# hi and lo of the activation side by side: one 512-column matmul in the transposed projections

## The chip, the cores and the metric

The kernel runs on one core of one Trainium2 chip. The metric is device time in microseconds, from a compiled program that is launched once per measurement. A profile gives one further execution with the start and the length of every instruction. In its rows PE is the TensorE matmul, PEld the weight load of TensorE, DVE the VectorE, ACT the ScalarE, POOL the GpSimd, and SP the SyncE, which here issues most DMAs.

## The reference

The reference is a network of two blocks over 256 tokens of width 1024, in float32. What matters here, cut down:

```python
# first block, layer 0 (even): three attentions over one input projection
qa, ka, va, qb, kb, vb, qm, gate = split_cols(h @ w_in_even[e], SPLIT_EVEN)
...
y = jnp.concatenate([ya, yb, ym], axis=-1) * jax.nn.silu(gate)
x = x + y @ w_out_even[e]
# layer 1 (odd): neighbourhood attention with 16 heads, and memory attention
qc, kc, vc, qm, gate = split_cols(h @ w_in_odd[o], SPLIT_ODD)
...
x = x + y @ w_out_odd[o]
# second block: mixer, cross attention, MLP
x = x + hybrid_mixer(rms_norm(x, g_mix), w_in, conv_w, g_attn_out, g_conv_out, w_out)
x = x + memory_cross_attention(rms_norm(x, g_xattn), rms_norm(mem, g_mem), w_q_mem, w_kv_mem, w_o_mem)
x = x + squared_relu_mlp(rms_norm(x, g_mlp), w_up, w_down)
return rms_norm(x, g_final)
```

Each `h @ w` is a product of 256 x 1024 with 1024 columns in, and between 512 and 4608 columns out. Two of these blocks keep memory keys and values (`mem @ w_kv`) as well.

## The kernel before, in words

**Split products.** Every operand of a large product is split in two float32r halves: hi is the value rounded, lo is the rest. A product is then made as hi·hi + hi·lo + lo·hi, three matmuls that accumulate in PSUM (`mm3`, line 421). For a weight, `split` (line 413) writes hi with a copy on ACT into a buffer `wh`, and lo with a subtraction on DVE into `wl`. Four buffers of each exist.

**Two kinds of projection.** `proj_n` (line 439) leaves the tokens on the partitions: the activation is the stationary operand, the split weight moves with up to 512 columns. `proj_t` (line 427) leaves the output columns on the partitions: 128 columns of the weight are stationary, the activation moves with all 256 tokens. It loads 256 weight columns for all eight k-tiles of 128 rows as one tile, and for each 128 columns (a block `f`) it splits 128 x 1024 weights and does eight times `mm3`. Both blocks of a call lie in one PSUM bank of 512 float32, and the readers read that bank directly.

**The activation.** hi and lo of an activation lie in tiles of [128, 4, 256], two for hi and two for lo, each with four k-tiles. A function `hT(l, k)` gives hi (l = 0) or lo (l = 1) of k-tile k. Four places make them: `gain_t` (line 478, tiles `gh`), `turns` (line 614, tiles `mT`), and in `layer_even` (line 985, tiles `hT`); `proj_n`, `proj_t` and `up_first` (line 1277) read them.

**Who reads a transposed projection.** `gate_tile` (line 769; a tanh on ACT, then a product on DVE), `q_stack` and `k_stack` (lines 649 and 661; halves for the heads), `mem_key` and `hilo` for the memory attention, the convolution in `mixer` (line 1177), the queries in `cross` (line 1238) and the squared relu of the MLP's `up` (line 1271).

**Memory.** Four PSUM banks bear the tag `mm` and four the tag `at`; projections use `mm`, except the MLP's `up` calls, which use `at`, as attention does. In SBUF a pool of 25 slots of 4 KB a partition (`SLOTS`) holds all larger activation tiles; work tiles have tags and counts of their own.

**Order.** The program is recorded first, then a planner orders it with costs per instruction (class `Plan`, `solve` at line 260): it takes, on each engine, the ready instruction that comes first in the program, moved by a few fixed shifts. Every instruction is then issued from line 284, so all rows of the profile name that line, and the tiles tell them apart. Attention heads are not called in place but queued in small steps; `pace` (line 330) lets some of them in after every four k-tiles of a projection, and `flush` does what is left before its result is needed. For a few operations, such as the scaling of softmax rows (`scaled`, line 601), the planner may choose between DVE and ACT.

**Stages.** In order of time: the even layer (normal projections for its keys and rotated queries, then eight and eight heads, and four memory heads), the odd layer (two groups of eight heads, four memory heads), the mixer (eight heads and a convolution), the cross attention (four heads of 256), the MLP (eight slices of 512 hidden columns, `up` of the next slice ahead of `down` of the current one). Keys and values of the second memory (`filling`, line 817) are put between stages.

Of the kernel before, what the change touches and what calls it, by code (L numbers as in the profile page):

```python
# [13 lines left out]
ALU = mybir.AluOpType  # L14
AX = mybir.AxisListType

P = 128
S = 256
D = 1024
KT = D // P  # L20
# [9 lines left out]
class Plan:  # L30
# [5 lines left out]
    class Engine:  # L36

        def __init__(self, plan, name):
            self.plan, self.engine = plan, name
# [244 lines left out]
            f(*[self.real(v) for v in args], **{k: self.real(v) for k, v in kwargs.items()})  # L284


class Kernel:

    def __init__(self, ctx, tc, a, out):
        self.tc, self.nc, self.a, self.out = tc, Plan(tc.nc), a, out  # L290

        class Pool:

            def __init__(pool, name, bufs, space=None):
                pool.space = space
                pool.real = ctx.enter_context(tc.tile_pool(name=name, bufs=bufs, **({"space": space} if space else {})))

            def tile(pool, shape, dtype, tag=None, name=None, bufs=1):
                return self.nc.tile(pool, shape, dtype, tag, name, bufs)

        pool = Pool
        self.base = pool("base", 1)
        self.wp = pool("wp", 4)
        self.wk = pool("wk", 2)
        self.bp = pool("bp", SLOTS)
        self.ps = pool("ps", 2, space=bass.MemoryType.PSUM)
        self.dr = pool("dr", 1, space=bass.MemoryType.DRAM)
        self.n = 0
        self.bg = deque()
        self.credit = 0.0  # L310
        self.rate = 0.0

    def name(self, s):
        self.n += 1
        return f"{s}_{self.n}"
# [4 lines left out]
    def slot(self, shape, name, dtype=F32R):  # L320
        return self.bp.tile(shape, dtype, tag="b4", name=self.name(name), bufs=SLOTS)

# [104 lines left out]
    def proj_t(self, w, c0, hT, n=256, tag="mm"):  # L427

        raw = self.load(w, 0, KT, c0, n)
        po = self.psum(tag)  # L430
        for f in range(n // P):
            wh, wl = self.split(raw[:, :, f * P:(f + 1) * P])
            for k in range(KT):
                self.mm3(po[:, f, :], wh[:, k, :], wl[:, k, :], hT(0, k), hT(1, k), k == 0, k == KT - 1)
                if k % 4 == 3:
                    self.pace()
        return po[:, :n // P, :]

    def proj_n(self, pieces, nk, n, hT, banks=None, start=True, stop=True):

        nc = self.nc
        po = banks or [self.psum("mm", [P, 512]) for _ in range(2)]
        for k0, view in pieces:
            wh, wl = self.split(view)
            for t in range(2):
                ts = slice(t * P, (t + 1) * P)
                for j in range(view.shape[1]):
                    k = k0 + j
                    o = po[t][:, :n]
                    xh, xl = hT(0, k)[:, ts], hT(1, k)[:, ts]  # L450
                    nc.tensor.matmul(o, xh, wh[:, j, :], start=start and k == 0, stop=False)
                    nc.tensor.matmul(o, xh, wl[:, j, :], start=False, stop=False)
                    nc.tensor.matmul(o, xl, wh[:, j, :], start=False, stop=stop and k == nk - 1)
                self.pace()
        return po
# [22 lines left out]
    def gain_t(self, src, key):  # L478

        nc = self.nc  # L480
        tiles = [[self.slot([P, 4, S], "gh") for _ in range(2)] for _ in range(2)]

        def turn(k):
            v, g, h, l = src[k // 4][:, k % 4, :], self.gcol(key, k), f(0, k), f(1, k)
            nc.scalar.activation(h, v, AF.Copy, scale=g)
            nc.vector.scalar_tensor_tensor(l, v, g, h.bitcast(F32), ALU.mult, ALU.subtract)

        f = lambda l, k: tiles[l][k // 4][:, k % 4, :]
        return f, turn

    def spread(self, r, b):

        nc = self.nc
        diag = self.work("p", [P, 2, P], PB)
        pb = self.psum("at")
# [83 lines left out]
    def mem_key(self, h, l, po, m):  # L579

        t = self.work("p", [P, 2, S], PB)
        self.nc.vector.tensor_tensor(t, po, m[2].unsqueeze(1).to_broadcast([P, 2, S]), ALU.mult)
# [23 lines left out]
    def square_sum(self, v, ms):  # L606

        junk = self.work("p", [P, 512], PB)
        self.nc.either(("scalar", "activation", (junk, v, AF.Square), {"scale": 1.0 / 32.0, "accum_out": ms}),
# [4 lines left out]
    def turns(self, tag, halves, key):  # L614

        nc = self.nc
        tiles = [[None, None], [None, None]]

        def turn(c, k2):
            if k2 == 0:  # L620
                for l in range(2):
                    tiles[l][c] = self.slot([P, 4, S], "mT")
            pt = self.psum("at")
            for j in range(2):
                k = 2 * k2 + j
                for t in range(2):
                    nc.tensor.transpose(pt[:, j, t * P:(t + 1) * P], halves[c][:, t, k * P:(k + 1) * P], self.ident)
            for j in range(2):
                k = 2 * k2 + j
                g = self.gcol(key, 4 * c + k)  # L630
                h, l = tiles[0][c][:, k, :], tiles[1][c][:, k, :]
                nc.scalar.activation(h, pt[:, j, :], AF.Copy, scale=g)
                nc.vector.scalar_tensor_tensor(l, pt[:, j, :], g, h.bitcast(F32), ALU.mult, ALU.subtract)

        for c in range(2):
            for k2 in range(2):
                self.later(tag, lambda c=c, k2=k2: turn(c, k2))
        return lambda l, k: tiles[l][k // 4][:, k % 4, :]


    def hilo(self, h, l, po, scale=1.0):
# [63 lines left out]
    def softmax(self, sc, bias=None, sink=None, causal=False):  # L705
# [3 lines left out]
        n = [P, S] if causal else [S, S]  # L709
        p = self.work("p", [P, 2, S], PB)  # L710
        st = self.work("st", [P, 8], 8)
# [39 lines left out]
    def pv_pair(self, ws, vs, causal=False):  # L751
# [4 lines left out]
        for e, ((ph, pl), v) in enumerate(zip(ws, vs)):  # L756
            for k in range(2):
                q = slice(P, S) if causal and k else slice(0, S)
                nc.tensor.matmul(po[:, e, q], v(k), ph[:, k, q], start=k == 0, stop=False)
                nc.tensor.matmul(po[:, e, q], v(k), pl[:, k, q], start=False, stop=k == 1)  # L760
        u = self.work("y", [P, S], YB)
        o = self.work("y", [P, S], YB)
        for e in range(2):
# [16 lines left out]
    def gated(self, y, f, o, g):  # L780
        nc = self.nc
        t = self.work("y", [P, S], YB)
        nc.vector.scalar_tensor_tensor(t, o, 0.5, g[:, f, :], ALU.mult, ALU.mult)
# [124 lines left out]
    def rope(self, tag, po, n, i, rx):  # L908
# [15 lines left out]
        def turn(t):  # L924
            src, r = po[t][:, :n * 64], rs[t]
            z = self.work("p", [P, 8, 64], PB)
            nc.vector.scalar_tensor_tensor(z[:, :n, :], src.rearrange("p (h c) -> p h c", c=64), rx[:, t:t + 1],
# [28 lines left out]
    def layer_even(self):  # L956
        nc, a = self.nc, self.a
# [20 lines left out]
        po = self.proj_n(pieces(), KT, 384, xg)  # L978
# [3 lines left out]
        nc.vector.tensor_tensor(sq[0], sq[0], sq[1], ALU.add)  # L982
        r = self.token_rms(sq[0])
        rb = self.spread(r, self.work("y", [P, S], YB))
        tiles = [[self.slot([P, 4, S], "hT") for _ in range(2)] for _ in range(2)]
        for c in range(2):
            t = self.slot([P, 4, S], "xs", F32)
            for k in range(4):
                nc.vector.scalar_tensor_tensor(t[:, k, :], self.xT[c][:, k, :], self.gcol("norm0", 4 * c + k), rb,
                                               ALU.mult, ALU.mult)  # L990
            for k in (0, 2):
                self.hilo(tiles[0][c][:, k:k + 2], tiles[1][c][:, k:k + 2], t[:, k:k + 2])
        hT = lambda l, k: tiles[l][k // 4][:, k % 4, :]
        self.window_bias()
        vs = []
        for c0 in (128, 256):
# [144 lines left out]
    def token_rms(self, sq):  # L1141

        nc = self.nc
        s = self.work("y", [P, S], YB)
        nc.vector.tensor_reduce(s, sq.rearrange("p r s -> p s r"), AX.X, ALU.add)
# [8 lines left out]
    def mixer(self, hT):  # L1154
# [22 lines left out]
        for i in range(2):  # L1177
# [8 lines left out]
            for f in range(2):  # L1186
                ff = 2 * i + f
                acc = self.work("y", [P, S], YB)
                tap = lambda j: self.gcol("convw", 4 * j + ff)
# [62 lines left out]
    def mlp(self, ms):  # L1252
# [11 lines left out]
        def square(t, f, n, po):  # L1264
            r = self.work("tanh", [P, 2, S], 2)[:, :n]
            nc.scalar.activation(r, po, AF.Relu)
            q = self.work("p", [P, 2, S], PB)[:, :n]
            nc.scalar.activation(q, r, AF.Square)
# [93 lines left out]
BIAS = [40, 80, 110, 0, 0]  # L1362
VERBOSE = False
LAG = (3, 1)
SLOTS = 25
YB = 5
PB = 4
PH = 4
IDLE = [1, 2, 1]
# [79 lines left out]
```

## Time and profile before

| | us |
|---|---|
| median of 3 runs | 787.56 (786.85 to 789.11) |
| the profiled execution | 786.07 |
| its span, first to last instruction | 784.3 |
| PE busy in it | 769.9 |
| DVE busy | 578.2 |
| ACT busy | 506.3 |
| POOL busy | 74.7 |

The mean granted TensorE clock is 0.997 of full speed. How to read the rows: a group's row names engine, operation, the tile written and the tiles read (buffer numbers left out), partitions by elements, a count; after the bar come the busy time of the group in us, the mean length of one in ns, and the idle time of the engine just before them with what ended it. A matmul's length runs to its modelled end in the pipeline, so the lengths of neighbours overlap; busy time counts the overlap once. A row of the waits names the waiting engine and tile, what it waited for, the total in us, the number of times and the longest. The share of 16 DMA engines that the main queue used is 52.0%.

### The profile page before, as it was taken

The page shows a single profiled execution, that of the slowest core. Times are in us where ns is not written, and L with a number is a line of the kernel's source. Part 1 is how long each engine was busy: PE and PEld are TensorE (multiplying, and loading weights), DVE is VectorE, ACT ScalarE, POOL GpSimd, SP SyncE. Part 2 cuts the span into 40 slices and gives each one's busy share as a digit, 9 for nine tenths or more (in the row PEclk, how much of TensorE's full clock was granted, in tenths as well). Part 3 has the DMA queues.
Part 4 walks back from the last instruction along what each step waited for, and adds up shares of the span by engine and source line. Part 5 has one row for each costly group of instructions (what it writes and reads, how often), then busy time and mean ns, then how long its engine had stood idle before and what let it go on. Part 6 is the DMA issues. An engine that isn't in the chain of part 4 may idle for free.

```text
span 784.3 us, 13568 instructions
## 1 busy us (share of the span) xinstructions
PE 769.9 (98%) x5320; PEld 715.2 (91%) x5320; DVE 578.2 (74%) x995; ACT 506.3 (65%) x928; POOL 74.7 (10%) x105
## 2 busy tenths in 40 slices
PE   7999999999999999999999999999999999999996
PEld 7799899888999999997999899799989999999985
DVE  5999988998769779869987788876567554445454
ACT  6687965975668568648785777465456654455452
POOL 0640010000001521132011000100000000000000
PEclk9999999999999999999999999999999999999999
DMA  7795455444468855773456644357435656565631
GB/s 229 243 333 163 161 166 195 151 159 164 161 198 260 220 175 156 196 233 135 151 172 191 187 159 164 107 162 242 161 108 168 201 170 203 171 208 170 205 116 54
DMA packets 109996, 140.60 MB, mean 179 GB/s; under 512 B 3779, under 2 KB 81539, under 8 KB 109932
## 3 DMA queue, kind: packets, MB, share of 16 engines
q1 hardware_dynamic: 104460, 131.64, 52.0%
q0 software_dynamic: 5472, 8.10, 4.6%
q8 instruction: 42, 0.69, 0.4%
q14 instruction: 22, 0.18, 0.1%
HBM read 134.98 MB, written 1.06 MB: 173 GB/s over the span
## 4 chain that ended last, share of the span: by engine, by line
PE 88%; DVE 4%; issue 3%; POOL 2%; DMA 1%; ACT 1%; SPq 0%; POOLq 0%; DVEq 0%; ACTq 0%
PE t_mm L284 66%; PE t_at L284 22%; DVE t_wl L284 1%; POOL t_rrs L284 1%; DMA t_xT<-in_x_t_dram 1%; DVE t_y L284 1%; DVE t_p L284 1%; POOL t_ks L284 1%; DMA t_tanh<-in_onehot_dram 0%; SPq L284 0%; ACT t_wh L284 0%; POOL t_rstd L284 0%; DVE t_gh L284 0%; DVE t_sq L284 0%; ACT t_tanh L284 0%
## 5 line engine op out<-in xcount | busy, mean ns | idle before, releaser
L284 DVE TENSOR_TENSOR t_wl<-t_raw,t_wh 128x1024 fp32r<-128x1024 f32 (+1 forms) x237 | 290.6, 1230 | 144.8 <-ACT t_wh L284 144.2
L284 ACT ACTIVATE t_wh<-t_raw 128x1024 fp32r<-128x1024 f32 (+1 forms) x237 | 249.0, 1055 | 200.1 <-PE t_mm L284 141.8
L284 PE MATMUL t_mm<-t_mT,t_wh 128*128 128x256 f32 x992 | 192.5, 287 | 0.0
L284 PEld LDWEIGHTS t_mm<-t_mT,t_wh 128*128 128x128 f32 x992 | 159.4, 191 | 0.4
L284 PE MATMUL t_mm<-t_mT,t_wl 128*128 128x256 f32 x496 | 141.1, 285 | 0.0
L284 PE MATMUL t_mm<-t_wh,t_yh 128*128 128x512 f32 x288 | 113.6, 395 | 0.0
L284 PE MATMUL t_mm<-t_wl,t_yh 128*128 128x512 f32 x288 | 113.6, 394 | 0.0
L284 PE MATMUL t_mm<-t_wh,t_yl 128*128 128x512 f32 x288 | 113.1, 394 | 0.0
L284 PE MATMUL t_at<-t_mT,t_wh 128*128 128x256 f32 x480 | 97.0, 282 | 0.0
L284 PEld LDWEIGHTS t_mm<-t_mT,t_wl 128*128 128x128 f32 x496 | 95.0, 191 | 0.0
L284 PEld LDWEIGHTS t_at<-t_mT,t_wh 128*128 128x128 f32 x480 | 78.8, 190 | 1.6
L284 PE MATMUL t_mm<-t_wh,t_gh 128*128 128x256 f32 (+2 forms) x256 | 65.6, 339 | 2.5 <-ACT t_wh L284 2.5
L284 PE MATMUL t_at<-t_mT,t_wl 128*128 128x256 f32 x240 | 67.6, 282 | 0.0
L284 PE MATMUL t_mm<-t_hT,t_wh 128*128 128x256 f32 x336 | 66.4, 287 | 0.0
L284 PEld LDWEIGHTS t_mm<-t_wh,t_yl 128*128 128x128 f32 x288 | 54.1, 188 | 10.6
L284 PEld LDWEIGHTS t_mm<-t_wl,t_yh 128*128 128x128 f32 x288 | 54.2, 188 | 10.0
L284 PEld LDWEIGHTS t_mm<-t_wh,t_yh 128*128 128x128 f32 x288 | 54.2, 188 | 9.7
L284 ACT ACTIVATE t_p<-t_p,t_st 128x256 f32<-128x256 f32 (+1 forms) x118 | 55.9, 490 | 7.4 <-DVE t_st L284 7.1
L284 POOL TENSOR_TENSOR t_rstd<-t_rstd,t_mhalf 128x2 f32<-128x2 f32 (+1 forms) x12 | 12.2, 1015 | 477.4 <-DVE t_rstd L284 477.4
L284 PEld LDWEIGHTS t_mm<-t_hT,t_wh 128*128 128x128 f32 x336 | 54.2, 191 | 0.3
L284 PE MATMUL t_mm<-t_gh,t_wh 128*128 128x256 f32 x256 | 51.1, 287 | 0.0
L284 PEld LDWEIGHTS t_mm<-t_wh,t_gh 128*128 128x128 f32 x256 | 44.6, 193 | 6.9 <-ACT t_wh L284 3.5
(173 smaller groups left out, 1317.6 us busy)
## 6 DMA issues: line engine op xcount, KB each, us to landing
t_raw<-in_w_in_odd_dram SPq DMA_DIRECT2D x20, 1024.0 KB, 5.1
t_raw<-in_w_up_dram SPq DMA_DIRECT2D x16, 1024.0 KB, 5.5
t_raw<-in_w_down_dram SPq DMA_DIRECT2D x16, 1024.0 KB, 5.2
t_raw<-in_w_in_dram SPq DMA_DIRECT2D x12, 1024.0 KB, 5.2
t_raw<-in_w_in_even_dram SPq DMA_DIRECT2D x10, 1024.0 KB, 5.2
t_raw<-in_w_mem_kv_dram SPq DMA_DIRECT2D x8, 1024.0 KB, 5.4
t_raw<-in_w_out_even_dram SPq DMA_DIRECT2D x6, 1024.0 KB, 5.0
t_raw<-in_w_out_odd_dram SPq DMA_DIRECT2D x6, 1024.0 KB, 5.1
```

What stands on the lines that cost most here:

```text
L284: f(*[self.real(v) for v in args], **{k: self.real(v) for k, v in kwargs.items()})
```

## The change

In every call of `proj_t`, the three matmuls of 256 columns per k-tile become two: one in which hi of the weights meets hi and lo of the activation side by side, 512 columns wide, and one in which lo of the weights meets hi of the activation, 256 columns wide. For that, hi and lo of the same k-tile must be neighbours in memory, so the activation tiles are now [128, 2, 2, 256]: two k-tiles, each with hi and lo. The class `Halves` makes and indexes them.

The wide matmul fills a whole PSUM bank with two partial sums. So each block of 128 output columns takes a bank of its own. When it is done, ACT copies the second half to a new work tile `sum` (two buffers of [128, 2, 256]), DVE adds the first half to it in place, and the readers of the projection get that tile, in SBUF, instead of the PSUM bank. `SLOTS` goes from 25 to 24. `up_first` and `proj_n` keep their matmuls and read the same tiles through the new indexing.

```diff
+class Halves:
+    def __init__(self, make):
+        self.make, self.tiles = make, {}
+    def pair(self, k):
+        if k // 2 not in self.tiles:
+            self.tiles[k // 2] = self.make()
+        t = self.tiles[k // 2]
+        return t[:, :, 0, :], t[:, :, 1, :]
+    def __call__(self, l, k):
+        return self.pair(k - k % 2)[l][:, k % 2, :]
+    def both(self, k):
+        self.pair(k - k % 2)
+        return self.tiles[k // 2][:, k % 2].rearrange("p l s -> p (l s)")
...
         self.rate = 0.0
+        self.merge = True
...
     def proj_t(self, w, c0, hT, n=256, tag="mm"):
         raw = self.load(w, 0, KT, c0, n)
+        if self.merge:
+            return self.proj_sum(raw, hT, n, tag)
...
+    def proj_sum(self, raw, hT, n, tag):
+        nc = self.nc
+        s = self.work("sum", [P, 2, S], SB)
+        for f in range(n // P):
+            wh, wl = self.split(raw[:, :, f * P:(f + 1) * P])
+            po = self.psum(tag)
+            pf = po.rearrange("p a b -> p (a b)")
+            for k in range(KT):
+                last = k == KT - 1
+                if last:
+                    nc.tensor.matmul(po[:, 0, :], wl[:, k, :], hT(0, k), start=False, stop=False)
+                nc.tensor.matmul(pf, wh[:, k, :], hT.both(k), start=k == 0, stop=last)
+                if not last:
+                    nc.tensor.matmul(po[:, 0, :], wl[:, k, :], hT(0, k), start=False, stop=False)
+                if k % 4 == 3:
+                    self.pace()
+            nc.scalar.copy(s[:, f, :], po[:, 1, :])
+            nc.vector.tensor_tensor(s[:, f, :], po[:, 0, :], s[:, f, :], ALU.add)
+        return s[:, :n // P, :]
...
     def gain_t(self, src, key):
-        tiles = [[self.slot([P, 4, S], "gh") for _ in range(2)] for _ in range(2)]
+        f = Halves(lambda: self.slot([P, 2, 2, S], "gh"))
...
     def turns(self, tag, halves, key):
-        tiles = [[None, None], [None, None]]
+        f = Halves(lambda: self.slot([P, 2, 2, S], "mT"))
...
-        tiles = [[self.slot([P, 4, S], "hT") for _ in range(2)] for _ in range(2)]
+        hT = Halves(lambda: self.slot([P, 2, 2, S], "hT"))
...
-SLOTS = 25
+SLOTS = 24
 YB = 5
+SB = 2
```

More of the change, by code (lines that the diff above doesn't have):

```diff
@@ L486, in turn @@
             nc.vector.scalar_tensor_tensor(l, v, g, h.bitcast(F32), ALU.mult, ALU.subtract)
-        f = lambda l, k: tiles[l][k // 4][:, k % 4, :]
         return f, turn
@@ L616, in turns @@
         nc = self.nc
-        tiles = [[None, None], [None, None]]
+        f = Halves(lambda: self.slot([P, 2, 2, S], "mT"))
         def turn(c, k2):
-            if k2 == 0:
-                for l in range(2):
-                    tiles[l][c] = self.slot([P, 4, S], "mT")
             pt = self.psum("at")
@@ L630, in turn @@
                 g = self.gcol(key, 4 * c + k)
-                h, l = tiles[0][c][:, k, :], tiles[1][c][:, k, :]
+                h, l = f(0, 4 * c + k), f(1, 4 * c + k)
                 nc.scalar.activation(h, pt[:, j, :], AF.Copy, scale=g)
@@ L637, in turns @@
                 self.later(tag, lambda c=c, k2=k2: turn(c, k2))
-        return lambda l, k: tiles[l][k // 4][:, k % 4, :]
+        return f
     def hilo(self, h, l, po, scale=1.0):
@@ L991, in layer_even @@
             for k in (0, 2):
-                self.hilo(tiles[0][c][:, k:k + 2], tiles[1][c][:, k:k + 2], t[:, k:k + 2])
-        hT = lambda l, k: tiles[l][k // 4][:, k % 4, :]
+                self.hilo(*hT.pair(4 * c + k), t[:, k:k + 2])
         self.window_bias()
```

## The prediction

> **What bounds the kernel now.** I read the busy times first, then the slices, to see whether one engine sets the pace everywhere.
>
> ```profile
> PE 769.9 (98%) x5320; PEld 715.2 (91%) x5320; DVE 578.2 (74%) x995; ACT 506.3 (65%) x928; POOL 74.7 (10%) x105
> ...
> PE   7999999999999999999999999999999999999996
> ...
> DVE  5999988998769779869987788876567554445454
> ```
>
> PE is busy in all slices but the first and the last. That alone proves little: a matmul is drawn from its start to its modelled end, about 280 ns for 256 columns, while the next one starts much earlier, so small stalls do not show. DVE has nine tenths in many slices of the first 500 us and only four to five tenths at the end. Averages over the span hide this, so the next view is busy time by stage: the even layer after its start, the odd layer, the mixer, the cross attention, the MLP (columns: PE, PEld, DVE, ACT, POOL in us with instruction counts, granted clock, DMA share, GB/s).
>
> ```profile
> 20.00:198.00 178.00, 176.03 (x1227) 162.23 (x1227) 158.66 (x321) 130.66 (x272) 24.11 (x36) 1.00 0.59 191
> 198.00:407.00 209.00, 207.76 (x1492) 195.35 (x1491) 170.24 (x316) 147.12 (x285) 38.98 (x45) 1.00 0.62 188
> 407.00:517.00 110.00, 109.79 (x791) 103.30 (x789) 89.08 (x170) 73.03 (x147) 7.82 (x12) 1.00 0.57 173
> 517.00:602.00 85.00, 85.00 (x629) 80.89 (x628) 56.48 (x82) 47.42 (x84) 0.59 (x1) 1.00 0.49 157
> 602.00:777.00 175.00, 175.00 (x1114) 158.80 (x1112) 89.65 (x92) 93.98 (x123) 1.26 (x2) 1.00 0.52 171
> ```
>
> DVE's share is 158.66/178 = 89% in the even layer, 81% in the odd layer and the mixer, 66% in the cross attention, 51% in the MLP. Two windows of 40 us show how full DVE gets while PE still runs:
>
> ```profile
> 60.00:100.00 40.00, 40.00 (x295) 37.70 (x293) 37.62 (x66) 32.19 (x74) 0.00 (x0) 1.00 0.53 173
> 360.00:400.00 40.00, 39.98 (x265) 36.64 (x266) 37.93 (x76) 31.64 (x69) 0.33 (x1) 1.00 0.51 163
> ```
>
> So PE sets the time, at a granted clock of 1.00, and in the even layer DVE is close behind. What lets PE run on is shown by the waits:
>
> ```profile
> ACT t_wh L284 <- PE t_mm L284: 141.8, 93, 3.2
> ```
>
> ACT stands 141.8 us in all because the weight buffers ahead of PE are still in use. In those places the splits of the weights are ahead of PE, by up to four buffers.
>
> **The matmuls.** The transposed projections are the matmuls of 256 columns that multiply a split weight by t_mT, t_hT or t_gh.
>
> ```profile
> L284 PE MATMUL t_mm<-t_mT,t_wh 128*128 128x256 f32 x992 | 192.5, 287 | 0.0
> L284 PE MATMUL t_mm<-t_mT,t_wl 128*128 128x256 f32 x496 | 141.1, 285 | 0.0
> L284 PE MATMUL t_at<-t_mT,t_wh 128*128 128x256 f32 x480 | 97.0, 282 | 0.0
> ...
> L284 PE MATMUL t_at<-t_mT,t_wl 128*128 128x256 f32 x240 | 67.6, 282 | 0.0
> L284 PE MATMUL t_mm<-t_hT,t_wh 128*128 128x256 f32 x336 | 66.4, 287 | 0.0
> L284 PE MATMUL t_mm<-t_gh,t_wh 128*128 128x256 f32 x256 | 51.1, 287 | 0.0
> L284 PE MATMUL t_mm<-t_hT,t_wl 128*128 128x256 f32 x168 | 48.0, 287 | 0.4 <-DVE t_wl L284 0.4
> ...
> L284 PE MATMUL t_mm<-t_gh,t_wl 128*128 128x256 f32 x128 | 36.9, 288 | 0.0
> ```
>
> The counts sum to 3096. up_first has the same form but is not changed: 2 x 2 x 2 x 4 x 3 = 96. That leaves 3000, which is 1000 groups of three or 125 blocks of eight groups. By the code they lie as 29 blocks in the even layer, 36 in the odd layer (32 and two fillers), 24 in the mixer, 8 in the cross attention, 28 in the MLP: 125 again. Per group, the change makes one matmul of 512 columns and one of 256 out of three of 256. The number of columns stays at 768; one instruction and one weight load go. What that is worth depends on the pace from start to start, not on the 287 ns of the rows above. I take the pace from stretches of the chain of waits in which PE waited for nothing (start, length, count):
>
> ```profile
> 409.07 22.55 PE t_mm L284 x188
> ```
>
> ```profile
> 755.45 16.36 PE t_mm L284 x72
> ```
>
> The first holds matmuls of 256 columns: 22.55/188 = 120.0 ns. The second holds the last down projection, 512 columns: 16.36/72 = 227.2 ns. Twice 256 columns cost 240.0, so merging saves 12.8 ns if the paces carry over to the new mix. The new mix alternates the sizes, and the trace has such a stretch, where attention was put between the matmuls of a normal projection:
>
> ```profile
> 88.07 0.28 PE L284 MATMUL t_at<-t_ph,t_vg 128*128 128x256 f32 x1
> 88.19 0.39 PE L284 MATMUL t_mm<-t_wh,t_gh 128*128 128x512 f32 x1
> ...
> 89.12 0.28 PE L284 MATMUL t_at<-t_pl,t_vg 128*128 128x256 f32 x1
> 89.23 0.39 PE L284 MATMUL t_mm<-t_wh,t_gh 128*128 128x512 f32 x1
> ```
>
> Between the first and the third line lie three pairs: 1.05/3 = 350 ns; between the second and the fourth also three: 1.04/3 = 347 ns. A group costs 360 now and 347 to 350 then, 10 to 13 ns less. I take 11.5. Times 1000 groups: **11.5 us** (10 to 13), namely 2.7 in the even layer, 3.3 in the odd, 2.2 in the mixer, 0.7 in the cross attention, 2.6 in the MLP.
>
> The Trainium skill says otherwise (TensorE: Matmul & The Clock Gate, Back-to-back issue gap): a warm matmul takes its columns over 2.4 GHz and about 2.5 ns more. By that, an estimate, the group would go from 327.6 to 325.0 ns, and the change would be worth 2.6 us. The rows of 120.0 and 227.2 ns do not agree; they leave some 13 ns beside the columns at both sizes. I go by the rows, and keep the page's case as a rival.
>
> **The added evacuation.** Each block now leaves two halves in one bank. ACT copies one half to the new tile, DVE adds the other to it, and the old readers read the tile. The nearest rows:
>
> ```profile
> L284 DVE TENSOR_TENSOR t_y<-t_mm,t_y 128x256 f32<-128x256 f32 x4 | 1.5, 419 | 0.2 <-PE t_mm L284 0.2
> ```
>
> ```profile
> L284 ACT ACTIVATE t_p<-t_tanh 128x512 f32<-128x512 f32 x14 | 8.8, 632 | 0.4
> ...
> L284 ACT ACTIVATE t_tanh<-t_mm 128x512 f32<-128x512 f32 x12 | 7.0, 587 | 1.6 <-DVE t_gate L284 1.3
> ...
> L284 ACT ACTIVATE t_tanh<-t_mm 128x256 f32<-128x256 f32 x2 | 0.8, 376 | 1.7 <-PE t_mm L284 1.7
> ```
>
> The DVE row is the same operation, PSUM and SBUF into SBUF: 125 x 419 ns = 52.4 us on DVE. The copy is 125 x 376 ns = 47 us on ACT. A reader on ACT that moves from PSUM to SBUF pays 632 - 587 = 45 ns more; with some 60 of them, under 3 us. Both engines have the room in sum (206 and 278 us idle), not everywhere:
>
> - MLP: 28 x 0.419 = 11.7 us into 85 us of idle DVE. Hidden. The projection's banks are wanted again only after a down projection of 48 matmuls, 48 x 0.227 = 10.9 us, against 0.8 us for copy and add. Cross attention: 3.4 into 28.5. Hidden. If that cover failed, each block would stand PE for up to 0.8 us.
> - Odd layer: 170.2 + 36 x 0.419 = 185.3 of 209, 89%. Mixer: 89.1 + 10.1 = 99.2 of 110, 90%. That is where the even layer stands now, so nearly hidden; I book 1 us for both together, between 0 and 3.
> - Even layer: 158.7 + 29 x 0.419 = 170.8 of 178, 96%. No stretch of 40 us has DVE over 37.93/40 = 94.8% now. At 94.8% the stage takes 170.8/0.948 = 180.2 us instead of 178: **+2.2 us, and its own 2.7 us of gain is lost**. One relief: the scaling of the softmax rows may be put on either engine by the planner.
>
> ```profile
> L284 DVE TENSOR_SCALAR t_p<-t_p,t_st 128x256 f32<-128x256 f32 x18 | 5.7, 347 | 0.2
> ```
>
> In the even layer 18 of these stand on DVE, 5.7 us. ACT there goes from 130.7 to 130.7 + 29 x 0.376 = 141.6 of 178 and could take them. With all of them gone DVE would stand at 165.1/178 = 93% and the stage would cost nothing: the lower bound. The upper bound is the rival below.
>
> **What moves.** hi and lo of two k-tiles now share a tile; the number of tiles is the same, and no DMA is added. The slots go from 25 to 24, for the two sum buffers. That slots are waited for can be read from issues that hang on work with no data for them:
>
> ```profile
> POOL t_wbias L284 <- DVE t_y L284: 48.0, 1, 48.0
> ...
> POOL t_gb L284 <- PE t_at L284: 26.4, 1, 26.4
> ```
>
> Both are loads fetched far ahead; I book 0.5 us and bound it by a rival. With two sum buffers, a copy for a third projection waits until the first has been read. Behind it on ACT stand the splits of the weights; four of these, at 8 x 0.35 us each, are 11 us of cover. Nothing booked.
>
> **Sum.** -11.5 + 2.7 + 2.2 + 1 + 0.5 = -5.1 us on the profiled execution's own 786.07 us (its span is 784.3, and 1.8 lies around it): 781.0. The median of the runs shown is 787.56, 1.5 above that execution; 787.56 - 5.1 = 782.5. **I predict 782.5 us.**
>
> **The rivals.**
>
> *DVE becomes the bound of the even layer* (slower). The even layer is a whole stage, not a stretch of 40 us, and no stage has DVE over 89.1% now. If that is the ceiling, the stage takes 170.8/0.891 = 191.7 us, +13.7, and the mixer 99.2/0.891 = 111.3, +1.3. Against that stand 3.3 + 0.7 + 2.6 = 6.6 us gained in the odd layer, cross attention and MLP: net +8.4, 796 us. The turning point: with 8.8 us gained outside the even layer, that stage may grow to 186.8 us, a DVE share of 170.8/186.8 = 91.4%. For it: one engine feeds PE with low halves of the weights and serves every softmax. Against it: 94% held over 60 to 100 us, and the scaling can move.
>
> *All of it is hidden*: -11.5, 776 us. It needs the scaling moved, and no cost at the places of the odd layer where DVE is at 94.8%.
>
> *The order suffers*: one slot less, and tiles that are read later, let a table or a load come one release later. Where the odd layer's second group of heads needs its bias tables, the trace already shows POOL standing until a gate has been read, for a small memset, and the tables right behind it (the waits by engine, then the order of time at 355 us):
>
> ```profile
> POOL t_tanh L284 <- DVE t_gate L284: 13.5, 1, 13.5
> ```
>
> ```profile
> 355.11 4.71 POOL L284 TENSOR_TENSOR t_rpbe<-t_cst,t_rpbraw 128x384 f32<-128x384 f32 x4
> ```
>
> A release that comes one gate tile later comes four blocks, 32 x 0.3485 = 11.2 us, later; if none of it is covered, -5.1 + 11.2 = +6.1, 793.5 us. Against it: out projections of 96 matmuls (96 x 0.227 = 21.8 us) stand there as cover.
>
> *The merged matmul saves nothing*: two halves at 120 ns each, as if the cost went by columns alone. Then 0 + 2.2 + 1 + 0.5 = +3.7, with the even layer at its own 178 us: 791 us. The stretch at 88.07 us speaks against it. The page named above would put this case at 3.7 - 2.6 = +1.1 us, 788.5.
>
> **How the numbers follow.** The forecast's case has 0.42 (its own range 779 to 786), all hidden 0.12, DVE as bound 0.26, the order 0.12, no saving 0.08. The range leaves out the far ends of the first and third: 776 to 795. A change of under 0.3%, 2.4 us, cannot be told from none. Faster: the 0.12 and 0.37 of the 0.42, 0.49. Within 0.3%: 0.05 of the forecast's case, 0.05 of the bound's milder forms, 0.06 of the last two, 0.16. Slower: 0.35.
>
> **What would show it.** 4320 matmuls, 1000 of the 512-column form with t_mT, t_hT or t_gh moving; pairs of 347 to 350 ns in the MLP, whose cycle shortens by 4 x 8 x 11.5 = 0.37 us; 125 copies near 376 ns and 125 sums near 419. The even layer's DVE share should end between 92 and 95%, with some of the scaling gone to ACT. I am wrong if the pair takes 355 ns or more, if the even layer ends over 3 us later, or if the odd layer's second heads come late.

## The result and the profile after

| | before | after |
|---|---|---|
| median, us | 787.75 (4 runs) | 779.58 (778.97 to 780.79, 4 runs) |
| ratio to before | | 0.991, 95% interval 0.9892 to 0.9929 |
| span of the profiled execution, us | 784.3 | 777.9 |

The kernel became 0.9% faster; 782.5 us was predicted for the median, and 779.58 was measured. The medians differ by 8.2 us, the two profiled executions by 6.4: the profiled execution of before, 786.07 us, was shorter than all four of its runs in the table (786.85 to 789.11). The rows of the page of the changed kernel that answer to those shown of before:

```profile
PE 763.1 (98%) x4320; PEld 661.2 (85%) x4320; DVE 620.0 (80%) x1127; ACT 536.8 (69%) x1046; POOL 74.7 (10%) x105
...
PE   8989999999999999999999999999999999999996
...
DVE  5999998998779889979988889976677655565554
```

A thousand matmuls and weight loads are gone, as counted. DVE is busy 41.8 us more and ACT 30.5, less than the new operations' lengths (125 x 0.421 = 52.6 and 125 x 0.371 = 46.4 us), since busy time counts the overlap of neighbours once: summed without that, the lengths of all instructions grew by 51.1 us on DVE and 46.1 us on ACT. The evacuation itself cost what its rows said, 376 and 419 ns (groups by form, changed kernel: count, busy us, mean ns, idle before):

```profile
L284 DVE TENSOR_TENSOR t_sum<-t_mm,t_sum 128x256 f32<-128x256 f32 x97 | 40.8, 421 | 13.5 <-ACT t_sum L284 12.7
...
L284 ACT COPY t_sum<-t_mm 128x256 f32<-128x256 f32 x97 | 36.0, 371 | 55.6 <-PE t_mm L284 55.1
```

Busy time by stage, in the changed kernel, with its own stage bounds (columns as in the prediction):

```profile
20.00:198.80 178.80, 175.03 (x995) 148.73 (x994) 166.73 (x348) 140.06 (x303) 24.16 (x36) 1.00 0.59 190
198.80:401.20 202.40, 202.40 (x1163) 175.91 (x1162) 176.38 (x353) 152.71 (x315) 37.62 (x45) 1.00 0.62 189
401.20:513.70 112.50, 111.81 (x642) 96.62 (x641) 100.76 (x198) 81.88 (x172) 8.96 (x12) 1.00 0.58 179
```

DVE's share is 166.73/178.80 = 93% in the even layer, 87% in the odd layer, 90% in the mixer.

**Where the time went.** A stage ends when PE has made the last transpose of the normalised activation for the next one. Two such ends, from the rows of those tiles (first and last start in us), before:

```profile
L284 PE MATMUL t_at<-t_cst,t_xn x16: 271/272/273, 198.6 to 200.3; 128*128 128x128 f32 x16
```

```profile
L284 PE MATMUL t_at<-t_cst,t_xg x16: 270/272/328, 406.6 to 408.8; 128*128 128x128 f32 x16
```

and after:

```profile
L284 PE MATMUL t_at<-t_cst,t_xn x16: 272/272/273, 199.4 to 201.1; 128*128 128x128 f32 x16
```

```profile
L284 PE MATMUL t_at<-t_cst,t_xg x16: 272/273/329, 401.0 to 403.0; 128*128 128x128 f32 x16
```

The even layer ends 0.8 us later; the odd layer takes 403.0 - 201.1 = 201.9 us instead of 208.5. The same reading for every kernel of this study, us in each stage of the profiled execution. It is one execution for each kernel, and the executions of one kernel lie between 0.4 us (wide_first) and 4.7 us (layout25) apart, so differences of under a microsecond in one of the first three stages mean little:

| kernel | even | odd | mixer | cross | MLP | span |
|---|---|---|---|---|---|---|
| before | 200.3 | 208.5 | 110.2 | 82.5 | 182.8 | 784.3 |
| after | 201.1 | 201.9 | 112.5 | 81.9 | 180.5 | 777.9 |
| layout24 | 200.5 | 208.5 | 110.1 | 82.5 | 182.9 | 784.5 |
| layout25 | 199.7 | 208.6 | 111.9 | 82.5 | 182.8 | 785.4 |
| evac_only | 203.8 | 206.5 | 113.1 | 82.4 | 182.9 | 788.7 |
| not_even | 199.6 | 202.7 | 112.5 | 81.9 | 180.5 | 777.3 |
| double_add | 203.0 | 203.2 | 114.6 | 82.0 | 180.7 | 783.4 |
| double_copy | 200.7 | 202.9 | 113.0 | 81.9 | 180.6 | 779.1 |
| sum4 | 201.0 | 202.2 | 112.4 | 81.9 | 180.5 | 778.1 |
| odd_cross_mlp | 200.3 | 202.2 | 112.2 | 82.0 | 180.5 | 777.1 |
| early_only | 202.8 | 202.7 | 114.1 | 82.0 | 180.5 | 782.1 |
| late_even | 198.1 | 202.7 | 112.5 | 81.9 | 180.5 | 775.7 |
| wide_first | 198.9 | 201.8 | 110.3 | 81.8 | 180.0 | 772.9 |
| wide_late | 198.6 | 203.0 | 110.4 | 81.8 | 180.3 | 774.1 |

The odd layer's 6.6 us overstate its gain and the mixer's 2.3 its loss, because work moved over their border. Before, the odd layer's window had 1489 matmuls and the mixer's 792 (198.6 to 407.0 and 407.0 to 517.2 us). The change takes 36 x 8 = 288 and 24 x 8 = 192 away, which leaves 1201 and 600; the rows above have 1163 and 642. Some 40 matmuls that stood in the odd layer now stand in the mixer. Taken together, the two stages went from 318.7 to 314.4 us, 4.3 less.

**The pace.** The MLP repeats one cycle with nothing else in it, so its period is the cleanest measure. Two rows of the chain of waits, four cycles apart, before:

```profile
643.02 4.33 PE t_mm L284 x19
...
732.96 4.33 PE t_mm L284 x19
```

and after:

```profile
635.08 7.50 PE t_mm L284 x33
...
643.95 2.82 PE t_at L284 x16
647.00 5.61 PE t_at L284 x32
...
723.72 7.51 PE t_mm L284 x33
```

A cycle took (732.96 - 643.02)/4 = 22.49 us and takes (723.72 - 635.08)/4 = 22.16. It holds 32 groups: 0.325 us over 32 is **10.2 ns a group**, where 11.5 was taken and 10 to 13 stated. The rows in between show pairs of a wide and a narrow matmul: 5.61/16 = 351 ns, 2.82/8 = 352 ns. Every matmul here has a weight load of its own, so the runs do not tell whether the saving belongs to the matmul or to the weight load that goes with it.

### The profile page after: what moved, and what is told of

It reads as the page before. It is cut to its first block, busy times and chain, and to the rows that moved or that the text cites. A ratio compares the mean times of both kernels' runs of the same rounds, so it can differ in the third digit from the quotient of the medians.

```text
span 777.9 us, 11758 instructions
## 1 busy us (share of the span) xinstructions
PE 763.1 (98%) x4320; PEld 661.2 (85%) x4320; DVE 620.0 (80%) x1127; ACT 536.8 (69%) x1046; POOL 74.7 (10%) x105
## 4 chain that ended last, share of the span: by engine, by line
PE 86%; DVE 5%; issue 3%; POOL 2%; ACT 2%; DMA 1%; SPq 0%; POOLq 0%; DVEq 0%; ACTq 0%
PE t_mm L284 64%; PE t_at L284 22%; DVE t_wl L284 2%; DVE t_y L284 1%; POOL t_rrs L284 1%; POOL t_rstd L284 1%; DMA t_xT<-in_x_t_dram 1%; POOL t_ks L284 1%; ACT t_wh L284 0%; DVE t_xs L284 0%; DVE t_p L284 0%; DVE t_x L284 0%; ACT t_p L284 0%; ACT t_xg L284 0%; ACT t_mT L284 0%
## 5 line engine op out<-in xcount | busy, mean ns | idle before, releaser
L284 PE MATMUL t_mm<-t_mT,t_wh 128*128 128x512 f32 (+1 forms) x512 | 181.6, 394 | 0.4 <-ACT t_wh L284 0.4
L284 PE MATMUL t_mm<-t_mT,t_wl 128*128 128x256 f32 x496 | 131.9, 284 | 0.0
L284 PEld LDWEIGHTS t_mm<-t_mT,t_wh 128*128 128x128 f32 x512 | 93.7, 188 | 14.0 <-ACT t_wh L284 0.8
L284 PE MATMUL t_at<-t_mT,t_wh 128*128 128x512 f32 (+1 forms) x256 | 85.7, 382 | 0.0
L284 ACT COPY t_sum<-t_mm 128x256 f32<-128x256 f32 x97 | 36.0, 371 | 55.6 <-PE t_mm L284 55.1
L284 PE MATMUL t_at<-t_mT,t_wl 128*128 128x256 f32 x240 | 63.8, 280 | 0.0
L284 PE MATMUL t_mm<-t_hT,t_wh 128*128 128x512 f32 x168 | 61.8, 400 | 1.0 <-DVE t_sum L284 1.0
L284 ACT ACTIVATE t_p<-t_p,t_st 128x256 f32<-128x256 f32 (+1 forms) x111 | 52.6, 493 | 9.6 <-DVE t_st L284 9.4
L284 PEld LDWEIGHTS t_at<-t_mT,t_wh 128*128 128x128 f32 x256 | 45.8, 188 | 6.8
L284 DVE TENSOR_TENSOR t_sum<-t_mm,t_sum 128x256 f32<-128x256 f32 x97 | 40.8, 421 | 13.5 <-ACT t_sum L284 12.7
```

## The experiments

The first question was whether the gain is PE's pace at all, or an order that the planner happened to find with new tiles and one slot less.

**layout24** keeps the new tiles and the slots and takes the merging out.

```diff
-        self.merge = True
+        self.merge = False
```

> The changed kernel with its three matmuls of 256 columns put back and without the sum tiles; the new activation tiles and the 24 slots stay. If the gain is TensorE's pace, this is the kernel before again: 785 to 789 us, with the odd layer within 2 us of its 208.5 us before. If the odd layer's 6.6 us came from the new tiles or the slots (a better order by chance), the odd layer stays near 202 us here and the whole is near 781 us.

Measured: 786.21 us, ratio to before 0.9992 (0.9981 to 1.0004), every stage within 0.2 us of before. Neither the tiles nor the slot moved anything.

**layout25** has the 25th slot as well.

```diff
-SLOTS = 24
+SLOTS = 25
```

> As layout24, with 25 slots. It separates the slot from the tiles: if one slot costs what was booked, 0.5 us, both are equal within the noise of 1 us; if slots matter to the order, this one is 2 us or more faster than layout24.

Measured: 786.68 us, ratio 1.0002 (0.999 to 1.0015). The slot is worth nothing. One thing to keep: the mixer took 111.9 us here and 110.1 in layout24, with the same matmuls and without any evacuation. That stage can differ by 1.8 us with no cause in the change; whether the order or the single execution makes the difference was not separated.

**evac_only** pays for the evacuation and gives up seven eighths of the merging.

```diff
-                nc.tensor.matmul(pf, wh[:, k, :], hT.both(k), start=k == 0, stop=last)
+                if k == 0:
+                    nc.tensor.matmul(pf, wh[:, k, :], hT.both(k), start=True, stop=False)
+                else:
+                    nc.tensor.matmul(po[:, 0, :], wh[:, k, :], hT(0, k), start=False, stop=False)
+                    nc.tensor.matmul(po[:, 1, :], wh[:, k, :], hT(1, k), start=False, stop=last)
```

> The changed kernel with its evacuation (copy on ACT, sum on DVE, a bank for each block), but seven of the eight wide matmuls of a block are two of 256 columns again. If the pace of TensorE is the gain, it costs 875 groups x 9 to 12 ns = 8 to 10 us over the changed kernel: 787 to 790 us, and the last stage, the MLP, takes about 182.5 us, as before. If merging saves nothing and the order does it all, it stays within 2 us of the changed kernel's 779.6.

Measured: 790.43 us, ratio 1.0039 (1.0024 to 1.0055), just above what the pace expects. From here to the changed kernel are 1.0039 - 0.991 = 1.3% or 10 us, and the only edit between them is that 875 wide matmuls are two narrow ones each. The planner's order may differ as well, but not in the MLP's cycle, which here reads

```profile
647.33 4.33 PE t_mm L284 x19
...
737.38 4.33 PE t_mm L284 x19
```

or 22.51 us, where the changed kernel has 22.16 and the kernel before 22.49. The gain is the pace. The evacuation with one eighth of the merging is a loss of 0.4%, and the MLP, at 182.9 us, shows almost none of it. Against before, the even layer is 3.5 us longer, and the odd layer and the mixer together 0.9 us (319.6 against 318.7).

**not_even** leaves the even layer out of the change.

```diff
-        self.merge = True
+        self.merge = False
...
         ms = self.layer_even()
+        self.merge = True
```

> The change in all stages but the even layer, which keeps three matmuls of 256 columns and reads PSUM directly; 24 slots. If the even layer lost because VectorE is full there, its end comes back from 201.1 to about 200.3 us and the whole ends 0.5 to 1.5 us under the changed kernel, 778 to 779. If its loss is small change of the order, the whole is within 1 us of it, on either side. If the even layer's own gain of pace (2.7 us) was in fact realised, this is 1 to 3 us slower, 781 to 782.

Measured: 779.62 us, ratio 0.9908 (0.9892 to 0.9924), the changed kernel's own time. The even layer came back to 199.6 us, the odd layer lost 0.8. So the change is worth nothing in the even layer: a pace of 29 x 8 x 10.2 ns = 2.4 us went in, and as much or somewhat more was lost. How much more can't be said to the microsecond: kernels whose even layer has no change of the matmuls end it between 199.6 and 200.5 us (before, layout24, layout25, not_even, odd_cross_mlp). Whether a full VectorE does that along the whole layer was the next question.

**double_add** and **double_copy** load one engine each with one more operation per block.

```diff
             nc.vector.tensor_tensor(s[:, f, :], po[:, 0, :], s[:, f, :], ALU.add)
+            nc.vector.tensor_tensor(s[:, f, :], s[:, f, :], s[:, f, :], ALU.max)
```

> The changed kernel with one more operation on VectorE after each sum (the maximum of the sum with itself, 128x256), 125 more in all, about 52 us of VectorE. If a full VectorE is what the evacuation costs, the even layer grows most: (166.7 + 12.2) us of VectorE at 95% are 188 us, some 5 to 10 us more, the mixer about 4 us more, the odd layer 0 to 3, cross attention and MLP nothing: 787 to 796 us in all. If only the delay from the last matmul to the reader counts, each stage grows by a few tenths of a microsecond for each place where it waits, and the whole by 3 us at most: under 783 us.

```diff
             nc.scalar.copy(s[:, f, :], po[:, 1, :])
+            nc.scalar.copy(s[:, f, :], po[:, 1, :])
```

> The changed kernel with the copy on ScalarE done twice, 125 more of 0.37 us, 46 us of ScalarE. The delay to the reader grows about as in double_add, but ScalarE has more room: (140 + 10.8)/179 = 84% in the even layer. If VectorE's fullness is the cause, this costs 0 to 3 us (up to 783); if the delay is the cause, it costs what double_add costs; if ScalarE is the engine that the evacuation fills, it costs more than double_add.

Measured: 785.45 us, ratio 0.9992 (0.9979 to 1.0005), with the second sum; 780.92, ratio 0.9931 (0.9918 to 0.9945), with the second copy. The first is under its expected 787 to 796: the even layer grew by 1.9 us, not 5 to 10. But it is above the 783 of the rival, and by the ratios the second sum cost 0.8% and the second copy 0.2%, though both delay a reader about alike. VectorE is the engine that counts, in the first three stages and not in the last two. Part of why it was less than expected is seen in the even layer's scaling of softmax rows on DVE (20 to 199 us), in the changed kernel:

```profile
L284 DVE TENSOR_SCALAR t_p<-t_p,t_st 128x256 f32<-128x256 f32 x16 | 5.1, 347 | 0.1
```

and in double_add:

```profile
L284 DVE TENSOR_SCALAR t_p<-t_p,t_st 128x256 f32<-128x256 f32 x8 | 2.5, 342 | 0.0
```

Eight more of them went to ACT. The change itself had moved only two (18 before). And DVE could be filled further than 94.8%, the most that any 40 us of before had shown: in double_add it is busy 96.61 of the 100 us from 60 to 160, with PE at 99.67 (columns: PE, PEld, DVE, ACT, POOL).

```profile
60.00:160.00 100.00, 99.67 (x600) 86.60 (x599) 96.61 (x214) 84.09 (x199) 3.90 (x5) 1.00 0.53 173
```

The time that PE's weight loads waited for lo of the weights grew, over the whole span, from

```profile
PEld t_mm L284 <- DVE t_wl L284: 4.4, 9, 1.4
```

in the changed kernel to this in double_add:

```profile
PEld t_mm L284 <- DVE t_wl L284: 9.9, 13, 2.1
```

Of the 5.5 us more, 3.5 lie in the mixer (405 to 520 us) and 0.8 in the first 64 us. A fuller DVE is felt where lo of the weights comes late.

**sum4** gives the evacuation four buffers.

```diff
-SLOTS = 24
+SLOTS = 23
...
-SB = 2
+SB = 4
```

> The changed kernel with four sum buffers instead of two, and 23 slots. If the wait of a copy for a sum tile that is still being read is what the mixer lost (110.1 us without the evacuation, 112.5 with it), the mixer comes back by 1 to 2 us: 777 to 778.5. If VectorE's fullness is what it lost, nothing changes: 779 to 780.5.

Measured: 780.91 us, ratio 0.993 (0.9918 to 0.9943), mixer 112.4: nothing came back. In the changed kernel's trace, too, every wait of a copy ended with a matmul, none with a reader of the tile.

**odd_cross_mlp** takes the even layer and the mixer out.

```diff
+        self.merge = True
         if upto > 1:
             ms = self.layer_odd(ms)
+        self.merge = False
...
+        self.merge = True
         if upto > 3:
             ms = self.cross(ms)
```

> The change only in the odd layer, the cross attention and the MLP; the even layer and the mixer, where the evacuation cost 3 us each and the pace gave back less, read PSUM as before. If the stages add up, the mixer takes 110 to 111 us, the odd layer about 202.5, and the whole is 777 to 778 us, 1.5 to 2.5 us under the changed kernel. If the stages' differences are accidents of the order that move elsewhere, it stays at 779 to 781.

Measured: 779.46 us, ratio 0.9914 (0.9901 to 0.9928): a miss. The mixer stayed at 112.2 us without any evacuation in it. Its 2.3 us need no evacuation, then. Its window (400.6 to 512.8 us) has 810 matmuls where before had 792, so work came over the border here as well; the rest can be the play that layout25 had shown, and was not separated.

**late_even** and **early_only** cut the even layer in two, after the first five blocks.

```diff
-        self.merge = True
+        self.merge = False
...
         g["a"] = self.gate_tile(w_in, 2048, hT)
+        self.merge = True
```

> The change everywhere but in the first five blocks of the even layer (keys of the windowed heads and the first gate, 33 to 60 us), which keep three matmuls of 256 columns and read PSUM. If the even layer's loss lies in those 30 us, where the trace shows TensorE waiting for VectorE and nothing else to do, the even layer ends near 198.5 us (199.6 with no block of it changed, less 24 x 8 x 9 ns = 1.7 us of pace, plus 0.6 us), and the whole is 776.5 to 778 us. If a full VectorE costs along the whole layer (60 to 160 us: 95% busy), the layer ends at 200 to 201 us and the whole is 779 to 780.

```diff
         g["a"] = self.gate_tile(w_in, 2048, hT)
+        self.merge = False
...
+        self.merge = True
         if upto > 1:
             ms = self.layer_odd(ms)
```

> The reverse inside the even layer: only its first five blocks are changed, the other 24 are not; all later stages are changed. If the loss lies in the first blocks, the layer ends at 201.5 to 202 us and the whole is 781 to 782. If it lies along the layer, the layer ends at 199.5 to 200 us, the whole at 779 to 780.

Measured: 777.48 us, ratio 0.9896 (0.9878 to 0.9913), even layer 198.1 us; and 782.91, ratio 0.9955 (0.994 to 0.9971), even layer 202.8 us. Against not_even's 199.6 us, the 24 later blocks gain 1.5 us of their 24 x 8 x 10.2 ns = 2.0, and the first five lose 3.2. Against the 200.3 us of odd_cross_mlp, whose even layer is the same program as not_even's, they gain 2.2 and lose 2.5; early_only's profiled execution, 783.87 us, was 1 us above its median, so the loss may be smaller still. By the ratios, early_only is 0.47% or 3.7 us slower than not_even, clear of both intervals; that late_even is 0.12% faster is not. In either reading, the even layer's loss sits in five of its 29 blocks. PE has little else to do there: 115 of the changed kernel's 138 matmuls between 33 and 60 us are those of the transposed projections, where from 60 to 160 us it is 287 of 605. Its timeline shows one such place (start, length, engine; idle time before and its releaser in brackets):

```profile
38.47 0.36 ACT L284 COPY t_sum<-t_mm 128x256 f32<-128x256 f32 x1
...
39.00 0.69 DVE L284 TENSOR_REDUCE t_rms<-t_tanh 128x8 f32<-128x512 f32 x1
...
39.72 0.42 DVE L284 TENSOR_TENSOR t_sum<-t_mm,t_sum 128x256 f32<-128x256 f32 x1
...
40.29 0.47 PE L284 MATMUL t_mm<-t_hT,t_wh 128*128 128x512 f32 x1 [1.02 <-DVE t_sum L284]
```

The copy is done at 38.83, but DVE is at work for the rotated heads and sums only at 39.72; the bank is free at 40.14, and PE has stood for it 1.02 us. Between 20 and 64 us, PE and its weight loads waited for lo of the weights as follows, before:

```profile
PEld t_mm L284 <- DVE t_wl L284: 0.9, 2, 0.6
...
PE t_mm L284 <- DVE t_wl L284: 0.4, 1, 0.4
```

and after:

```profile
PEld t_mm L284 <- DVE t_wl L284: 3.0, 6, 1.4
...
PE t_mm L284 <- DVE t_wl L284: 1.2, 2, 1.0
PE t_mm L284 <- DVE t_sum L284: 1.0, 1, 1.0
```

In the same window, late_even is near before again (1.3 and 0.5 us, and no wait for a sum), and early_only has 4.1, 2.1 and 1.0. That the evacuation brings these waits, and not the width of the matmuls, is seen over the whole span of evac_only (4.0, 1.6 and 1.0 us, against 1.9, 0.8 and none in layout24). Later, DVE is as full and it costs little: this window of the changed kernel (columns PE, PEld, DVE, ACT, POOL) has it busy for 94.70 of 100 us, and the blocks there lose 0.5 us at most by the figures above.

```profile
60.00:160.00 100.00, 99.76 (x605) 87.52 (x604) 94.70 (x203) 83.68 (x196) 2.94 (x4) 1.00 0.52 170
```

**wide_first** puts the narrow matmuls of a block behind seven of the wide ones. Lo of the weights is then needed later, and the width changes twice in a block instead of fourteen times.

```diff
+            def wide(k):
+                nc.tensor.matmul(pf, wh[:, k, :], hT.both(k), start=k == 0, stop=k == KT - 1)
+            for k in range(KT - 1):
+                wide(k)
+                if k == 3:
+                    self.pace()
+            for k in range(KT):
+                nc.tensor.matmul(po[:, 0, :], wl[:, k, :], hT(0, k), start=False, stop=False)
+            wide(KT - 1)
+            self.pace()
```

> The changed kernel with the matmuls of a block in another order: seven wide ones, then the eight narrow ones with lo of the weights, then the last wide one. If the change of width costs (a wide matmul took about 233 ns before a narrow one and 227 before a wide one in the changed kernel's trace), a block saves up to 7 x 3 to 6 ns, 2.5 to 5 us in all: 775 to 777. If it doesn't, nothing changes there, and only the waits for lo of the weights (5 to 6 us in the changed kernel's profile, most of them in the first 60 us) can shrink, since lo is needed 1.6 us later: 777.5 to 779.5.

Measured: 774.37 us, ratio 0.9847 (0.9832 to 0.9863), better than both kernels and under the 775 to 777 expected. Both effects came. The MLP's cycle, again four cycles apart:

```profile
630.38 7.49 PE t_mm L284 x33
...
718.76 7.49 PE t_mm L284 x33
```

That is 22.10 us instead of 22.16, 2 ns a group, 2 us over the kernel's 1000 groups. And the weight loads' wait for lo, 4.4 us in the changed kernel, shrank:

```profile
PEld t_mm L284 <- DVE t_wl L284: 1.2, 2, 0.7
```

The even layer is 2.2 us shorter and the mixer 2.2. The mixer's share of the pace is 0.4 us, and the weight loads' wait for lo there was only 0.3; the rest of its gain has no cause shown and is of the size of the play in that stage.

**wide_late** joins the two best.

> wide_first and late_even together: the wide matmuls first, and the first five blocks of the even layer unchanged from before. If wide_first took its time in the even layer from the same waits in the first blocks that late_even avoids, little is left to gain: the layer ends at 198 to 198.5 us (198.9 in wide_first, 198.1 in late_even), the whole is 773 to 774.5. If the two are independent, the layer ends near 196 us and the whole is 771 to 772.

Measured: 774.88 us, ratio 0.9857 (0.984 to 0.9875), even layer 198.6, both just above the first case's 773 to 774.5 and 198 to 198.5: nothing added. Once lo is needed later, leaving the first blocks out brings no more.

## Why the prediction was right, point by point

- **PE's pace sets the time, and merging saves a fixed part per instruction: right.** 10.2 ns a group in the MLP, at the low end of the stated 10 to 13, so 10.2 us instead of 11.5. The pair was taken at 348.5 ns, the middle of the readings; with 120.0 for a narrow one alone, the cycle says 360 - 10.2 = 349.8. evac_only shows the cause: with 875 of the 1000 wide matmuls split again, 10 us go. By the formula that the Trainium skill gives for an isolated warm matmul (TensorE: Matmul & The Clock Gate, Back-to-back issue gap), the saving is estimated at 2.5 ns a group, 2.5 us in all (the prediction's 2.6 comes of rounding). The measured 10.2 ns a group decides against it for these matmuls.
- **The evacuation's durations: right**, 421 and 371 ns against 419 and 376.
- **MLP and cross attention hide it: right.** They gained 2.3 and 0.6 us, predicted 2.6 and 0.7, and doubling either operation there cost 0.2 us at most.
- **Odd layer and mixer, -5.5 + 1 us: right as a sum**, -4.3 against -4.5. That the sum fits to 0.2 us is partly luck, as the mixer alone varied by 1.8 us between layout24 and layout25. Neither alone was predicted (-6.6 and +2.3), since matmuls crossed their border.
- **The even layer, 2.2 us longer and its own gain lost: right in sign, wrong in the mechanism.** The step that failed is the ceiling of 94.8% for DVE over the whole stage. It ended 0.8 us longer (within the 0.9 us between kernels with the same matmuls there), which is 3.2 us lost against its pace where 4.9 was booked. The runs put 2.5 to 3.2 us of loss into the five blocks between 33 and 60 us, where PE has little other work; with DVE at 94.70% from 60 to 160 us, the later 24 blocks lose 0.5 us at most. The load was mis-sized too: the 12.2 us of sums raised DVE's busy time in the stage from 158.66 to 166.73 us, not to 170.8, and 166.73/0.948 is 175.9 us, so that with the load as it came the ceiling would have asked for nothing. The relief by moved scaling, named beside it, hardly occurred: 18 on DVE became 16.
- **The slot, 0.5 us: nothing**, by layout24 and layout25.
- **The rivals.** DVE as bound over the stage would have needed 796 us; double_add shows that even 12 us more DVE work in the even layer stretch it by 1.9 only, with DVE at 96.61% for 100 us. "The merged matmul saves nothing" fell with the MLP's cycle, "the order suffers" with layout24.

In sum -10.2 + 3.2 + 0.6 = -6.4 us, the change of the span, against -5.1 predicted: the gain was 1.3 us smaller and the losses 2.6 us smaller than written. The two errors partly cancel. The median moved further, by 8.2 us; the 1.8 us beyond the profiled executions is spread between executions that no term of the sum stands for.

## What to carry to other kernels

Where one engine's instructions follow each other without a gap, count instructions as well as elements: here a narrow matmul took 120.0 ns and a wide one 227.2, so each, with its weight load, carried 2 x 120.0 - 227.2 = 12.8 ns beside its columns, if a column costs the same in both. The evacuation onto a nearly full engine cost most, in this kernel, where the bound engine had little other work, not where the busy share was highest; look for that place stage by stage. And when a split product's lo half comes from the busy engine, use it late in the accumulation: here that cut the weight loads' wait for it from 4.4 to 1.2 us.

## What the runs showed of the hardware

The time from one matmul's start to the next depends on the widths of both. In the changed kernel's trace its median was 233 ns for 512 columns before 256 (906 cases) and 227 ns for 512 before 512 (1155 cases), while 256 before 512 took 117 ns (913 cases) and 256 before 256 took 120 (819 cases). A change there and back costs 233 + 117 - 227 - 120 = 3 ns. wide_first has 2 changes in a block where the changed kernel has 14; by this estimate the six pairs fewer are worth 18 ns a block, or 2.2 ns a group, and its MLP took 2 ns less a group. What in the chip causes it was not tried.
